# A two-layer decoder trunk on one core: seven-product cases of the last down-projection placed in another order, fed from other buffers, and the end of the last norm written in another order

## The chip, the cores and the metric

The kernel runs on one core of a Trainium2 chip. The metric is the device time of one execution in microseconds (us). Three runs of the kernel before took 2057.11, 2058.33 and 2062.94 us; the median is 2058.33 us.

The engines are named as the profile names them: PE multiplies matrices, PEld is its loading of weights, DVE and ACT do element-wise work, POOL is hardly used here, and SP issues nearly all the transfers (DMAs) from device memory, in order. The chip's memory on the core is 128 partitions wide; a "128x512" tile has 512 numbers of four bytes in each partition. PE sums its products in eight PSUM tiles ("ps", 128x512 each).

## The reference, cut to what matters

Two layers act on 256 tokens of width 2048 (`x`). The change concerns the last step of the second layer, its gated feed-forward network, and the final norm behind it:

```python
D_MODEL, D_FF = 2048, 5632
def conv_ffn(h, w_up, cw, cb, w_down):
    a = h @ w_up                                   # 256 x 2048 by 2048 x 11264
    c = (causal depthwise convolution of width 3 over the tokens of a) + cb
    gate, val = c[..., :D_FF], c[..., D_FF:]
    return (jax.nn.silu(gate) * val) @ w_down      # 256 x 5632 by 5632 x 2048
...
    x = x + conv_ffn(rmsnorm(x, g_ffn[l]), w_ffn_up[l], conv_w[l], conv_b[l], w_ffn_down[l])
return rmsnorm(x, g_final)
```

Everything is in 32-bit floats. `w_down` alone is 5632 x 2048 numbers, 46 MB, and is read once.

## The kernel before, in words

**Two parts for each number.** [...] The high part is a rounded copy (ACT, L702 and L715), the low part is the raw number minus the high one (DVE, L703 and L716). A product of two tiles is three matmuls: high by high, high by low, low by high (`three`, L751 to L753).

**Thirds, halves, cases.** The feed-forward network of layer 1 goes over its 5632 features in thirds of 2048, 2048 and 1536 (`FF_GROUPS = (4, 4, 3)`, in groups of 512). Each third first computes its features (up-projection, convolution, SiLU gate, product) and then multiplies them by its rows of `w_down` and adds the result to the residual stream. That second step, `down_phase`, is where the change lies. It runs twice per third, for the left and the right 1024 columns of the output (`ph` 0 and 1; the text calls them halves). In a half, the work is cut into cases: a case `k` is 256 features, and its weights are two tiles `x` and `y` of 128x1024 floats (512 KB each), loaded by SP (L766). A half has 8 cases in the first two thirds and 6 in the last.

**Plain and seven-product cases.** The output of a half is 256 tokens by 1024 columns, four quarters of 128x512: `e00`, `e01` (first 128 tokens, left and right columns), `e10`, `e11` (second 128 tokens). A plain case adds 8 products (24 matmuls of 128x512) to them. A seven-product case ("fast" in the code) uses sums of its weight quarters and sums of its feature quarters, in the manner of Strassen, and needs 7 products (21 matmuls). Three of them go to `e00`, `e01`, `e10`; four go to accumulators of their own, `m1`, `m5`, `m6`, `m7`, which ACT copies out behind the last such case of a half (`between`, L1332), and which DVE adds into the result later (`combine`, recorded as L1340). The sums of weights are made on DVE: `xs` of 512 columns each (L725, L726, L728, L729) and one low part of 512 (`we`, L722), beside three low parts of 1024 columns (L716). A plain case has two low parts of 1024 (L703) and no sums.

**What sets the order.** `FF_FAST` names the seven-product cases and, for each half, the order of the cases. The order of instructions on PE, DVE and ACT then comes from a scheduler that simulates the program, except in the last half, where `late=2` cases are kept back and the rest is written out by hand (`manual_schedule`). Weight tiles as loaded ("raw") live in a ring of 4 buffers; SP issues a load when the buffer's last reader is done, and the loads behind it wait in SP's queue. High and low parts live in rings too. The eight PSUM tiles of a half are used by the next half once they are read out.

**The end of a half.** `evict(tb, half, ...)` adds the quarter of token block `tb` to the residual `xt` (L1359, DVE). In the last third it also sums the squares (L1375, ACT), multiplies by the gain (L1379, DVE), and behind the last quarter of a token block finishes the norm: small operations on one column (L1381 to L1393), then the scaling of the block's 2048 columns (L1396 on ACT, L1397 and L1398 on DVE), and its output (L1399 to L1401). In the last half the first token block's quarters are evicted, its norm finished and its output issued, all ahead of the second token block's evictions; the very last quarter `e11` goes in two pieces of 256 columns.

Of the kernel before, what the change touches and what calls it, by code (L numbers as in the profile page):

```python
# [34 lines left out]
    4: ((2, 3, 4), ((0, 1, 2, 5, 3, 6, 4, 7), (2, 0, 3, 1, 4, 5, 6, 7))),  # L35
    3: ((1, 2), ((0, 1, 3, 2, 4, 5), (1, 0, 2, 3, 4, 5))),
# [37 lines left out]
class Kernel:  # L74
# [632 lines left out]
    def fast_pair(self, raws, pool):  # L707
# [10 lines left out]

        b21, b22 = parts(y)
# [4 lines left out]
        t13, t24 = sums  # L724
        tt(t13[:, left], x[:, left], x[:, right], ALU.add)  # L725
        tt(t13[:, right], x[:, right], y[:, right], ALU.add)  # L726
        t1, t3 = parts(t13)
        tt(t24[:, left], t13[:, left], y[:, right], ALU.add)  # L728
        tt(t24[:, right], t24[:, left], y[:, left], ALU.add)  # L729
        t2, t4 = parts(t24)  # L730
        return b21, b22, b11, t1, t3, t4, t2


    def down_phase(self, dn, col, order, fast, lhs, rhs, pool, between, evict, late=0):
        mm = self.nc.tensor.matmul
        first_fast = order[0] in fast
        names = ("m1", "m5", "m6", "m7"), ("e00", "e01", "e10", "e11")
        acc = {n: self.psum() for group in (names if first_fast else names[::-1]) for n in group}
# [23 lines left out]
        for n, k in enumerate(order):  # L762
            raws = []
            for i in range(2):
                raw = self.wp.tile([P, 1024], F32, tag="raw", name=self.uid("raw"), bufs=4)
                self.nc.sync.dma_start(out=raw, in_=dn[(2 * k + i) * P : (2 * k + i + 1) * P, col : col + 1024])  # L766
                raws.append(raw)
            if k in fast:
                names7 = "e00", "e01", "m1", "m5", "m7", "e10", "m6"
                for name, q, w in zip(names7, (1, 6, 0, 4, 3, 2, 5), self.fast_pair(raws, pool)):  # L770
# [3 lines left out]
            else:  # L774
# [5 lines left out]
                else:  # L780
                    for half in range(2):
                        plain(k, ws, 0, half)
# [7 lines left out]
        with self.tc.manual_schedule(engines={ET.PE, ET.DVE, ET.Activation}):  # L790
            for half in range(2):
                evict(0, half, acc[f"e0{half}"])
            for k, ws in kept:
                plain(k, ws, 1, 0)
            evict(1, 0, acc["e10"])
            for k, ws in kept[:-1]:
# [8 lines left out]
            evict(1, 1, rest, 1)  # L805


    def ffn(self, l, after=None, to_tokens=None, tokens=None):
# [5 lines left out]
        with self.tc.tile_pool(name=self.uid("ff"), bufs=1) as fp:  # L814
            g0 = 0
            for part, ng in enumerate(FF_GROUPS):
                h = self.ap.tile([P, NB * 512], F32R, tag="big", name=self.uid("h"))
                last = part == len(FF_GROUPS) - 1
                fast, orders = FF_FAST[ng] if tokens is not None else ((), None)
                if tokens is None:  # L820
                    plain = {k: h[:, 1024 * k : 1024 * (k + 1)] for k in range(2 * ng)}
                else:
                    places = [h[:, o : o + 1024] for o in range(1792 * len(fast), NB * 512 - 1023, 1024)]
# [4 lines left out]
                    split7 = {k: h[:, 1792 * i : 1792 * (i + 1)].rearrange("p (s q) -> p s q", s=2) for i, k in enumerate(fast)}  # L828
# [12 lines left out]
                for g in range(g0, g0 + ng):  # L841
# [6 lines left out]
                    def ev(b, acc):  # L848
# [21 lines left out]
                        d = split7[n // 2]  # L870
# [557 lines left out]
```

## Time and profile before

| | |
|---|---|
| median of three runs | 2058.33 us (2057.11 to 2062.94) |
| the profiled execution | 2055.74 us, of which the span of the profile is 2054.0 us |
| PE busy | 2033.3 us, 99% of the span |
| DVE busy | 1508.9 us, 73% |
| ACT busy | 1115.4 us, 54% |
| weight tiles of `w_ffn_down` | 176 transfers of 512 KB (half of them in layer 1) |
| down-projections of layer 1 | 1497 to 1583 us, 1757 to 1843 us, 1974 to 2040 us |

A row of the timeline has the start and the length of an instruction (us), engine, source line, operation, the tile written and the tiles read, and in brackets the idle time ahead of it and what ended it. Matmuls are pipelined: their lengths overlap, and the distance between starts tells the pace. Rows that are merged ("x2") have one start and one total length. In a view of stretches each row has the stretch, its length, the busy time of PE, weight load, DVE, ACT and POOL (with counts), the granted PE clock, the share of the DMA engines and GB/s.

### The profile page before, as it was taken

The page shows a single profiled execution, that of the slowest core. Times are in us where ns is not written, and L with a number is a line of the kernel's source. Part 1 is how long each engine was busy: PE and PEld are TensorE (multiplying, and loading weights), DVE is VectorE, ACT ScalarE, POOL GpSimd, SP SyncE. Part 2 cuts the span into 40 slices and gives each one's busy share as a digit, 9 for nine tenths or more (in the row PEclk, how much of TensorE's full clock was granted, in tenths as well). Part 3 has the DMA queues.
Part 4 walks back from the last instruction along what each step waited for, and adds up shares of the span by engine and source line. Part 5 has one row for each costly group of instructions (what it writes and reads, how often), then busy time and mean ns, then how long its engine had stood idle before and what let it go on. Part 6 is the DMA issues. An engine that isn't in the chain of part 4 may idle for free.

```text
span 2054.0 us, 39946 instructions
## 1 busy us (share of the span) xinstructions
PE 2033.3 (99%) x16226; PEld 1962.6 (96%) x16226; DVE 1508.9 (73%) x2286; ACT 1115.4 (54%) x1613; POOL 142.0 (7%) x200
## 2 busy tenths in 40 slices
PE   9999999999999999999999999999999999999996
PEld 8989999999999999999999999999987999879995
DVE  5866767767656766467788787777787777878788
ACT  6754744555435555345545675455555555555564
POOL 0000013000000000000042242300000000000000
PEclk9999999999999999999999999999999999999999
DMA  8876566666666666666665534668755666566663
GB/s 248 234 215 184 165 194 190 194 194 194 195 195 190 197 194 193 195 195 195 194 191 181 179 119 160 190 199 214 215 192 188 204 195 196 185 196 205 195 210 119
DMA packets 233821, 394.68 MB, mean 192 GB/s; under 512 B 53854, under 2 KB 61348, under 8 KB 233508
## 3 DMA queue, kind: packets, MB, share of 16 engines
q1 hardware_dynamic: 233444, 391.58, 63.4%
q8 instruction: 127, 2.08, 0.4%
q10 hardware_dynamic: 192, 0.54, 0.1%
q14 instruction: 58, 0.48, 0.1%
HBM read 387.88 MB, written 2.10 MB: 190 GB/s over the span
## 4 chain that ended last, share of the span: by engine, by line
PE 90%; DVE 5%; DMA 3%; ACT 1%; issue 1%; DVEq 0%; ACTq 0%; SPq 0%
PE ps L156 25%; PE ps L157 25%; PE ps L159 25%; DMA raw<-in_w_ffn_down 3%; PE ps L188 2%; PE ps L190 2%; PE ps L189 2%; PE ps L752 1%; PE ps L753 1%; PE ps L751 1%; DVE wlo L703 1%; PE ps L523 1%; DVE wlo L716 1%; DVE xs L728 0%; DVE xt L1359 0%
## 5 line engine op out<-in xcount | busy, mean ns | idle before, releaser
L118 DVE TENSOR_TENSOR wlo<-raw,whi 128x1024 fp32r<-128x1024 f32 x572 | 710.3, 1245 | 392.5 <-ACT whi L117 387.8
L117 ACT ACTIVATE whi<-raw 128x1024 fp32r<-128x1024 f32 x572 | 606.5, 1062 | 703.1 <-PE ps L157 591.4
L156 PE MATMUL ps<-xhl,whi 128*128 128x256 f32 x3264 | 762.7, 277 | 0.0
L157 PE MATMUL ps<-xhl,whi 128*128 128x256 f32 x3264 | 761.1, 276 | 0.0
L157 PEld LDWEIGHTS ps<-xhl,whi 128*128 128x128 f32 x3264 | 612.8, 188 | 0.3
L156 PEld LDWEIGHTS ps<-xhl,whi 128*128 128x128 f32 x3264 | 612.7, 188 | 0.3
L159 PE MATMUL ps<-xhl,wlo 128*128 128x256 f32 x3264 | 436.6, 276 | 0.0
L159 PEld LDWEIGHTS ps<-xhl,wlo 128*128 128x128 f32 x3264 | 400.5, 188 | 0.0
L156 PE MATMUL ps<-h,whi 128*128 128x256 f32 x704 | 163.6, 276 | 0.0
L157 PE MATMUL ps<-h,whi 128*128 128x256 f32 x704 | 163.6, 276 | 0.0
L157 PEld LDWEIGHTS ps<-h,whi 128*128 128x128 f32 x704 | 132.0, 188 | 0.0
L156 PEld LDWEIGHTS ps<-h,whi 128*128 128x128 f32 x704 | 131.8, 188 | 0.0
L156 PE MATMUL ps<-mainhl,whi 128*128 128x256 f32 x512 | 119.6, 277 | 0.0
L157 PE MATMUL ps<-mainhl,whi 128*128 128x256 f32 x512 | 119.3, 276 | 0.0
L835 ACT ACTIVATE c<-a,cT 128x256 f32<-128x256 f32 x176 | 99.5, 589 | 9.8 <-DVE a L236 9.7
L157 PEld LDWEIGHTS ps<-mainhl,whi 128*128 128x128 f32 x512 | 96.0, 188 | 0.0
L156 PEld LDWEIGHTS ps<-mainhl,whi 128*128 128x128 f32 x512 | 95.9, 188 | 0.0
L159 PE MATMUL ps<-h,wlo 128*128 128x256 f32 x704 | 94.1, 276 | 0.0
L752 PE MATMUL ps<-wlo,h 128*128 128x512 f32 (+1 forms) x226 | 88.3, 391 | 1.9 <-DVE wlo L703 1.9
L753 PE MATMUL ps<-whi,h 128*128 128x512 f32 (+1 forms) x226 | 87.5, 387 | 0.0
L122 ACT ACTIVATE whi<-raw,gT 128x512 fp32r<-128x512 f32 x96 | 63.9, 716 | 42.2 <-PE ps L157 21.4
L236 DVE TENSOR_TENSOR a<-ps,rbc 128x256 f32<-128x256 f32 x176 | 69.8, 418 | 23.0 <-PE ps L159 23.0
(368 smaller groups left out, 2738.2 us busy)
## 6 DMA issues: line engine op xcount, KB each, us to landing
raw<-in_w_ffn_up SPq DMA_DIRECT2D x352, 512.0 KB, 4.3
raw<-in_w_ffn_down SPq DMA_DIRECT2D x176, 512.0 KB, 4.4
raw<-in_w_out SPq DMA_DIRECT2D x64, 512.0 KB, 4.6
raw<-in_w_in_a SPq DMA_DIRECT2D x56, 512.0 KB, 4.4
raw<-in_w_mem_kv SPq DMA_DIRECT2D x31, 512.0 KB, 4.7
raw<-in_w_in_b SPq DMA_DIRECT2D x16, 512.0 KB, 4.3
raw<-in_w_kv_a SPq DMA_DIRECT2D x9, 512.0 KB, 5.4
raw<-in_w_uq SPq DMA_DIRECT2D x12, 384.0 KB, 3.0
```

The source lines that it names most:

```text
L117: nc.scalar.activation(hi[:, :n], raw[:, :n], AF.Copy)
L118: nc.vector.tensor_tensor(lo[:, :n], raw[:, :n], hi[:, :n].bitcast(F32), ALU.subtract)
L122: nc.scalar.activation(hi[:, s], raw[:, s], AF.Copy, scale=gains[k])
L156: mm(acc[:, :S], wh, x[:, :S], start=first, stop=False)
L157: mm(acc[:, :S], wh, x[:, S:], start=False, stop=False)
L159: mm(acc[:, :S], wl, x[:, :S], start=False, stop=last)
L188: mm(acc, xh, wh, start=first, stop=False)
L189: mm(acc, xh, wl, start=False, stop=False)
L236: self.nc.vector.tensor_tensor(out, acc[:, :S], r, ALU.mult)
L752: mm(o, xh, wl, start=False, stop=False)
L753: mm(o, xl, wh, start=False, stop=stop)
L835: nc.scalar.activation(c, a, AF.Identity, scale=w(2), bias=w(3))
```

## The change

It has six parts, all of them in the down-projection of layer 1's feed-forward network.

1. `FF_FAST`: 15 seven-product cases where there were 16. In the first two thirds the cases 2, 3, 4 stay, and both halves now run in the order 0, 1, 2, 5, 3, 6, 7, 4. In the last third the left half keeps cases 1 and 2 (order 0, 1, 3, 2, 4, 5); the right half has case 1 alone, in the order 0 to 5, and case 2 is a plain case there, whose features come from the quarters that are kept for the left half.
2. Raw tiles: a seven-product case takes its two weight tiles from the ring "gate" of two buffers, which also holds the gate tiles of the up-projection. Only the first seven-product case of each left half and all plain cases take them from the ring "raw" of four.
3. The four sums come first on DVE in a seven-product case, ahead of its low parts.
4. The seven products run in the order `e00, e01, e10, m6, m5, m7, m1` (before: `e00, e01, m1, m5, m7, e10, m6`), and the accumulators are always taken in the order `e` then `m`.
5. The scaling and the output of a token block are a function of their own, `finish`. In the last half `finish(0)` is called behind the eviction of `e10`, the second token block's left quarter.
6. In the last half the two kept cases now bring all their products behind the other cases: both cases' `e00`, eviction, both cases' `e01`, eviction, both cases' `e10`, eviction, then `e11`. Before, `e00` and `e01` of each kept case ran as the case came.

PE has 13705 rows after and 13702 before, DVE 2144 and 2151, ACT 1437 and 1439, SP 769 both.

**DVE where the left half of the first third ends and the right half begins.** `ps_18752` to `ps_18755` are the left half's quarters, whose L1359 (after: L1372) are the evictions. Before, raw_19176 and raw_19178 are the weights of the right half's case 3, wlo_19116 belongs to its case 2, and wlo_19145 to its plain case 0:

```order
L725 TENSOR_TENSOR xs_19180<-raw_19176 128x512
L716 TENSOR_TENSOR wlo_19116<-xs_19099,whi_19115 128x1024
L1359 TENSOR_TENSOR xt<-ps_18752,xt 128x512
L722 TENSOR_TENSOR we_19186<-raw_19176,we_19186 128x512
L726 TENSOR_TENSOR xs_19180<-raw_19176,raw_19178 128x512
L1359 TENSOR_TENSOR xt<-ps_18753,xt 128x512
L728 TENSOR_TENSOR xs_19181<-xs_19180,raw_19178 128x512
L1359 TENSOR_TENSOR xt<-ps_18754,xt 128x512
L1359 TENSOR_TENSOR xt<-ps_18755,xt 128x512
L703 TENSOR_TENSOR wlo_19145<-raw_19140,whi_19144 128x1024
```

After, gate_19166 and gate_19168 are the weights of the right half's case 2, wlo_19054 is the last low part of the left half's case 4, and wlo_19099 and wlo_19103 are those of the right half's first case, the plain case 0:

```order
L716 TENSOR_TENSOR wlo_19054<-xs_19036,whi_19053 128x1024
L721 TENSOR_TENSOR xs_19170<-gate_19166,gate_19168 128x512
L1372 TENSOR_TENSOR xt<-ps_18755,xt 128x512
L722 TENSOR_TENSOR xs_19171<-xs_19170,gate_19168 128x512
L1372 TENSOR_TENSOR xt<-ps_18752,xt 128x512
L703 TENSOR_TENSOR wlo_19099<-raw_19094,whi_19098 128x1024
L1372 TENSOR_TENSOR xt<-ps_18753,xt 128x512
L1372 TENSOR_TENSOR xt<-ps_18754,xt 128x512
L723 TENSOR_TENSOR xs_19171<-xs_19171,gate_19168 128x512
L703 TENSOR_TENSOR wlo_19103<-raw_19096,whi_19102 128x1024
```

The half now begins with a plain case, and two sums of a later case stand between the last low part of one half and the first of the next.

**SP's queue in the left half of the last third.** The names 24110 and 24112 are case 3, 24146 and 24148 case 2, 24196 and 24198 case 4, 24232 and 24234 case 5; higher numbers belong to the right half. Before:

```order
L766 DMA raw_24110<-in_w_ffn_down 128x1024
L766 DMA raw_24112<-in_w_ffn_down 128x1024
L766 DMA raw_24146<-in_w_ffn_down 128x1024
L766 DMA raw_24148<-in_w_ffn_down 128x1024
L766 DMA raw_24196<-in_w_ffn_down 128x1024
L766 DMA raw_24198<-in_w_ffn_down 128x1024
L766 DMA raw_24232<-in_w_ffn_down 128x1024
L766 DMA raw_24234<-in_w_ffn_down 128x1024
```

After (case 2's first tile, gate_24146, stands earlier, out of this piece):

```order
L768 DMA raw_24110<-in_w_ffn_down 128x1024
L768 DMA raw_24112<-in_w_ffn_down 128x1024
L768 DMA raw_24196<-in_w_ffn_down 128x1024
L768 DMA raw_24198<-in_w_ffn_down 128x1024
L768 DMA raw_24232<-in_w_ffn_down 128x1024
L768 DMA raw_24234<-in_w_ffn_down 128x1024
L768 DMA gate_24148<-in_w_ffn_down 128x1024
L768 DMA gate_24334<-in_w_ffn_down 128x1024
```

Case 2's second tile has moved behind the tiles of the cases 4 and 5, which run after it.

**DVE around case 2 of that half, after.** gate_23460 is the last gate tile of the up-projection, whose last reader is L863 (before: L854), and gate_24148 takes its buffer; L245 is the low part of the features:

```order
L727 TENSOR_TENSOR we_24160<-gate_24146,we_24160 128x512
L863 TENSOR_TENSOR hv_24013<-gate_23460,c_24009 128x256
L245 TENSOR_TENSOR h_22333<-hv_24013,h_22333 128x256
L721 TENSOR_TENSOR xs_24150<-gate_24146,gate_24148 128x512
L722 TENSOR_TENSOR xs_24151<-xs_24150,gate_24148 128x512
L716 TENSOR_TENSOR wlo_24157<-gate_24148,whi_24156 128x1024
```

The load of gate_24148 now comes between the second row and the fourth.

**DVE in the last half's end.** Before, `ps_24295` is the first token block's second quarter, `ps_24296` and `ps_24297` are the second token block's quarters:

```order
L1359 TENSOR_TENSOR xt<-ps_24295,xt 128x512
L1387 TENSOR_SCALAR fv<-fsums,fpart 128x1
L1391 RECIPROCAL froot<-froot 128x1
L1392 SCALAR_TENSOR_TENSOR fq<-froot,fv 128x1
L1393 SCALAR_TENSOR_TENSOR froot<-fq,froot 128x1
L1397 TENSOR_SCALAR xt<-xt,froot 128x512
L1398 SCALAR_TENSOR_TENSOR xt<-xt,froot,gb 128x512
L1359 TENSOR_TENSOR xt<-ps_24296,xt 128x512
L1379 TENSOR_TENSOR xt<-xt,gb 128x512
L1381 TENSOR_REDUCE fpart<-fsums 128x1
L1382 TENSOR_SCALAR fpart<-fpart 128x1
L1359 TENSOR_TENSOR xt<-ps_24297,xt 128x256 x2
```

After (`ps_24291`, `ps_24292`, `ps_24293` are the same three):

```order
L1372 TENSOR_TENSOR xt<-ps_24291,xt 128x512
L1400 TENSOR_SCALAR fv<-fsums,fpart 128x1
L1404 RECIPROCAL froot<-froot 128x1
L1405 SCALAR_TENSOR_TENSOR fq<-froot,fv 128x1
L1406 SCALAR_TENSOR_TENSOR froot<-fq,froot 128x1
L1372 TENSOR_TENSOR xt<-ps_24292,xt 128x512
L1392 TENSOR_TENSOR xt<-xt,gb 128x512
L1394 TENSOR_REDUCE fpart<-fsums 128x1
L1395 TENSOR_SCALAR fpart<-fpart 128x1
L1412 TENSOR_SCALAR xt<-xt,froot 128x512
L1413 SCALAR_TENSOR_TENSOR xt<-xt,froot,gb 128x512
L1372 TENSOR_TENSOR xt<-ps_24293,xt 128x256 x2
```

The two scalings of the first block have moved behind the second block's first quarter.

The diff, cut to its core:

```diff
 FF_FAST = {
-    4: ((2, 3, 4), ((0, 1, 2, 5, 3, 6, 4, 7), (2, 0, 3, 1, 4, 5, 6, 7))),
-    3: ((1, 2), ((0, 1, 3, 2, 4, 5), (1, 0, 2, 3, 4, 5))),
+    4: (((2, 3, 4), (0, 1, 2, 5, 3, 6, 7, 4)), ((2, 3, 4), (0, 1, 2, 5, 3, 6, 7, 4))),
+    3: (((1, 2), (0, 1, 3, 2, 4, 5)), ((1,), (0, 1, 2, 3, 4, 5))),
 }
...
+        t13, t24 = sums
+        tt(t13[:, left], x[:, left], x[:, right], ALU.add)
+        tt(t13[:, right], x[:, right], y[:, right], ALU.add)
+        tt(t24[:, left], t13[:, left], y[:, right], ALU.add)
+        tt(t24[:, right], t24[:, left], y[:, left], ALU.add)
         b21, b22 = parts(y)
         one = self.tmp(pool, [P, 1040], "we", 1, F32R)[:, :1024]
...
-        t13, t24 = sums
-        tt(t13[:, left], x[:, left], x[:, right], ALU.add)
-        tt(t13[:, right], x[:, right], y[:, right], ALU.add)
+        t2, t4 = parts(t24)
         t1, t3 = parts(t13)
-        tt(t24[:, left], t13[:, left], y[:, right], ALU.add)
-        tt(t24[:, right], t24[:, left], y[:, left], ALU.add)
-        t2, t4 = parts(t24)
-        return b21, b22, b11, t1, t3, t4, t2
+        return b21, b22, t4, t2, t1, t3, b11
...
-        first_fast = order[0] in fast
-        acc = {n: self.psum() for group in (names if first_fast else names[::-1]) for n in group}
+        acc = {n: self.psum() for group in names[::-1] for n in group}
...
-                raw = self.wp.tile([P, 1024], F32, tag="raw", name=self.uid("raw"), bufs=4)
+                if k in fast and (col or k != fast[0]):
+                    raw = self.tmp(fp, [P, 1024], "gate", 2)
+                else:
+                    raw = self.wp.tile([P, 1024], F32, tag="raw", name=self.uid("raw"), bufs=4)
...
-                names7 = "e00", "e01", "m1", "m5", "m7", "e10", "m6"
-                for name, q, w in zip(names7, (1, 6, 0, 4, 3, 2, 5), self.fast_pair(raws, pool)):
+                names7 = "e00", "e01", "e10", "m6", "m5", "m7", "m1"
+                for name, q, w in zip(names7, (1, 6, 2, 5, 4, 3, 0), self.fast_pair(raws, pool)):
...
                 else:
-                    for half in range(2):
-                        plain(k, ws, 0, half)
                     kept.append((k, ws))
...
             for half in range(2):
+                for k, ws in kept:
+                    plain(k, ws, 0, half)
                 evict(0, half, acc[f"e0{half}"])
             for k, ws in kept:
                 plain(k, ws, 1, 0)
             evict(1, 0, acc["e10"])
+            finish(0)
...
             evict(1, 1, rest, 1)
+            finish(1)
...
-            y, rows = xt[:, tb, :], slice(tb * P, (tb + 1) * P)
-            for a in (512, 1024):
-                nc.scalar.activation(y[:, a : a + 512], y[:, a : a + 512], AF.Copy, scale=one(r))
+
+    def finish(self, tb):
+        nc, y, rows, r = self.nc, self.xt[:, tb, :], slice(tb * P, (tb + 1) * P), self.r[:, tb : tb + 1]
+        for a in (512, 1024):
+            nc.scalar.activation(y[:, a : a + 512], y[:, a : a + 512], AF.Copy, scale=r)
```

What is left out of the diff: the features of the last third's case 2, which stay whole there (1024 columns of quarters where a seven-product case keeps 896) so that the right half can use them as a plain case; and the rest of `finish`, which is the old end of `evict` as it was.

36 lines of the change are left out of this document (22 added, 14 removed).

## Prediction

> **What bounds the kernel now.** I read the page first (busy shares, chain), then the stretches of the three down-projections, then PE's waits, then the timeline where the longest waits lie.
>
> ```profile
> span 2054.0 us, 39946 instructions
> PE 2033.3 (99%) x16226; PEld 1962.6 (96%) x16226; DVE 1508.9 (73%) x2286; ACT 1115.4 (54%) x1613; POOL 142.0 (7%) x200
> PE 90%; DVE 5%; DMA 3%; ACT 1%; issue 1%; DVEq 0%; ACTq 0%; SPq 0%
> ```
>
> PE is busy for 99%: the time is PE's matmuls, its few waits, and what lies behind the last matmul. Ahead of the first down-projection nothing is changed.
>
> ```profile
> 1496.93:1583.31 86.38, 84.43 (x369) 68.31 (x368) 71.86 (x92) 47.70 (x59) 0.00 (x0) 1.00 0.59 191
> 1757.40:1842.94 85.54, 84.38 (x369) 68.32 (x367) 71.94 (x92) 47.93 (x59) 0.00 (x0) 1.00 0.58 192
> 1973.51:2040.26 66.75, 64.41 (x284) 51.60 (x282) 62.27 (x86) 38.92 (x57) 0.00 (x0) 1.00 0.43 141
> ...
> 1567.15 0.91 PE ps L751 x4
> ...
> 2040.02 0.28 PE L752 MATMUL ps<-wlo,h 128*128 128x256 f32 x1
> 2040.14 0.28 PE L753 MATMUL ps<-whi,h 128*128 128x256 f32 x1
> ```
>
> A 128x512 matmul takes 0.91/4 = 0.2267 us, a 256-wide one 2040.14 - 2040.02 = 0.12 us. A third has 6x21 + 10x24 = 366 matmuls, 82.97 us without a wait, so the first two stretches hold 3.4 and 2.6 us of waits; the last has 270 wide and 12 narrow ones, 62.65 us, so 4.1 us. In all 10.1 us, and behind the last matmul 2054.0 - 2040.14 = 13.86 us. These two sums are all that the change can take from, beside the matmuls themselves.
>
> ```profile
> PE ps L751 <- DVE xt L1359: 1.9, 2, 1.2
> PE ps L752 <- DVE wlo L703: 1.9, 4, 0.6
> PE ps L751 <- ACT staged L1332: 0.7, 1, 0.7
> PE ps L751 <- ACT whi L715: 0.7, 2, 0.5
> PE ps L751 <- ACT whi L702: 0.3, 1, 0.3
> ```
>
> PE waits for DVE most: for evictions (L1359) and low parts (L703). DVE is 72 of 86 us busy in a stretch, so it has slack but is late in places.
>
> **The matmuls.** One seven-product case less: 24 - 21 = 3 matmuls, +0.68 us, all on the path. DVE loses one case's four sums and `we`, less than it has to spare; the plain case's features come from the quarters that exist, so ACT and DVE copy 128 columns more, which lies under the up-projection's matmuls. The new order of the sums inside a case moves no work between engines.
>
> **The border between halves, first two thirds.**
>
> ```profile
> 1541.15 0.39 PE L751 MATMUL ps<-we,h 128*128 128x512 f32 x1
> 1542.79 0.50 PE L751 MATMUL ps<-whi,h 128*128 128x512 f32 x1 [1.24 <-DVE xt L1359]
> ...
> 1540.30 0.69 DVE L725 TENSOR_TENSOR xs<-raw 128x512 f32<-128x512 f32 x1 [2.79 <-DMA raw<-in_w_ffn_down]
> 1542.05 0.68 DVE L1359 TENSOR_TENSOR xt<-ps,xt 128x512 f32<-128x512 f32 x1
> 1545.05 1.28 DVE L1359 TENSOR_TENSOR xt<-ps,xt 128x512 f32<-128x512 f32 x2
> 1546.25 2.35 DVE L703 TENSOR_TENSOR wlo<-raw,whi 128x1024 fp32r<-128x1024 f32 x2
> ```
>
> PE stands still before 1542.79 because an eviction at 1542.05 is late; it stands in DVE's queue behind L725, which waited 2.79 us for a raw tile. This wait goes: the right half now begins with two plain cases, and its first seven-product case has buffers of its own. What is late next: the order of after puts, between the left half's last low part and the right half's first, two sums and two evictions, 4 x 0.6 us (start of L1359 to start of L703 here: 1.20 for two), then the low part, 1.13 us (2.35 less overlap, for two): 3.6 us. In that time PE has the last low part's remaining products, about 8 matmuls, 1.8 us. So PE waits 1.8 us, restarts cost about 0.1 each (the row of 0.50 in place of 0.39), and case 4, now last with its sums and evictions close, about 0.9 later in the half: 3.2 us in a third, 6.4 for both, against 3.4 + 2.6 = 6.0. Term: +0.4. Ends: -4 (the sums slip into idle time, no border wait: 1.8 x 2 and restarts) and +4 (DVE starts none of the 3.6 us ahead of PE's need).
>
> **Case 2 of the last third's left half.** Its second tile is moved in SP's queue behind the tiles of cases 4 and 5 and takes the buffer of the last gate tile, which is free when L854 has read it.
>
> ```profile
> 1985.35 0.68 DVE L729 TENSOR_TENSOR xs<-xs,raw 128x512 f32<-128x512 f32 x1
> 1985.95 1.22 DVE L703 TENSOR_TENSOR wlo<-raw,whi 128x1024 fp32r<-128x1024 f32 x1
> ...
> 1988.41 1.22 DVE L716 TENSOR_TENSOR wlo<-raw,whi 128x1024 fp32r<-128x1024 f32 x1
> 1990.68 0.42 DVE L854 TENSOR_TENSOR hv<-gate,c 128x256 f32<-128x256 f32 x1
> ...
> 1989.86 0.61 PE L751 MATMUL ps<-whi,h 128*128 128x512 f32 x2
> ...
> raw<-in_w_ffn_down SPq DMA_DIRECT2D x176, 512.0 KB, 4.4
> ...
> L702 ACT ACTIVATE whi<-raw 128x1024 fp32r<-128x1024 f32 x55 | 57.4, 1055 | 22.2 <-PE ps L157 8.0 <-PE ps L753 5.9 <-DMA raw<-in_w_ffn_down 3.7
> ```
>
> The last L854 ran at 1990.68, with case 2's sums and low parts ahead of it. After, these can't be, since their tile comes later: three sums at 0.6 and two low parts at 1.13 are 4.1 us, less some 0.4 of idle time and a low part of features ahead of it: the product ends near 1987.0. The load takes 4.4 us, to 1991.4; the high part 1.06, to 1992.5. PE needs it at 1989.86: it waits 2.6 us. Then the case runs at DVE's pace: low part of `y` to 1993.6 (PE waits 0.9 after one matmul), third sum and high part of `t24` to 1995.3 (0.5 to 0.8), its low part to 1996.4 (0.9). PE has done 12 matmuls at 1997.6 in place of 1989.86 + 12 x 0.2267 = 1992.6: 5.0 us. Behind it the order has two sums of the right half's case 1 ahead of case 4's low part: 0.9 more; restarts 0.5: 6.4 us. For the rest of the stretch I keep 1.2 us, since the right half has one seven-product case and most of DVE's slack: 7.6 us against 4.1. Term: +3.5. Queued behind the held load on SP are the tiles of the right half's case 1 alone, needed some 11 us later, so nobody else waits. Ends: +1 (the product is done 1 us sooner and the load takes 3.2) and +6 (it isn't done sooner than 1988 and the load takes 5).
>
> **The end.**
>
> ```profile
> 2036.77 0.69 DVE L1359 TENSOR_TENSOR xt<-ps,xt 128x512 f32<-128x512 f32 x1 [1.22 <-PE ps L753]
> ...
> 2039.11 0.68 DVE L1359 TENSOR_TENSOR xt<-ps,xt 128x512 f32<-128x512 f32 x1
> ...
> 2041.71 0.49 DVE L1397 TENSOR_SCALAR xt<-xt,froot 128x512 f32<-128x512 f32 x1
> 2042.11 0.75 DVE L1398 SCALAR_TENSOR_TENSOR xt<-xt,froot,gb 128x512 f32<-128x512 f32 x1
> 2042.78 0.68 DVE L1359 TENSOR_TENSOR xt<-ps,xt 128x512 f32<-128x512 f32 x1
> ...
> 2045.11 0.74 DVE L1359 TENSOR_TENSOR xt<-ps,xt 128x256 f32<-128x256 f32 x2
> ...
> 2046.74 0.48 DVE L1371 CUSTOM_DVE_ANT_0 fjunk<-xt,fpart 128x256 f32<-128x256 f32 x1
> ...
> 2049.57 0.38 ACTq L1401 DMA_DIRECT2D out_y<-xt  x1
> ```
>
> With E for the last matmul's start, 2040.14: the last sum of squares is at E + 6.6, and from there to the end it is 7.26 us, 4.4 of them the last output. DVE takes the first quarter at E - 3.4 and the second block's first at E + 2.64 only, although PE finished it before E: the first block's chain, with L1397 and L1398, stands ahead. After, a quarter's two kept cases are 12 matmuls, 2.7 us; `e11` has 6 x 0.2267 + 12 x 0.12 = 2.8. So `e10` is done at E - 2.8, `e01` at E - 5.5, `e00` at E - 8.2, and DVE takes each as it comes: `e10` at E - 2.35 and its small work to E - 0.0 (2.33 us, 2042.78 to 2045.11 here), then the first block's scaling to E + 1.05 (1.07 us, 2041.71 to 2042.78), then the last quarter's pieces (1.63 us, 2045.11 to 2046.74): the last sum of squares at E + 2.7 in place of E + 6.6. Term: -3.9. Ends: -4.5 (scaling done while DVE would wait) and -2 (the first block's output, now nearer to the second's, holds it up).
>
> **The sum.** +0.68 + 0.4 + 3.5 - 3.9 = +0.7. The profiled execution took 2055.74 us, 1.74 of them around the span, and is 2.6 us below the median of the runs. On the median: 2058.33 + 0.7 = 2059.0 us.
>
> **Rivals.**
>
> *A hidden load, a quiet border (faster).*
>
> ```profile
> L725 DVE TENSOR_TENSOR xs<-raw 128x512 f32<-128x512 f32 x16 | 11.1, 691 | 12.3 <-DMA raw<-in_w_ffn_down 12.3
> ```
>
> Two buffers of their own let SP fetch a seven-product case's tiles without waiting for the plain ring; now DVE waits 12.3 us for them ahead of L725, which speaks for it. If the borders' waits go (6.0 to 2.4) and case 2 is no later than now: 0.68 - 3.6 + 0 - 3.9 = -6.8, 2051.5 us. Against it: the buffer of case 2's tile is held by L854, as the order shows.
>
> *The two buffers hold up every half (slower).* A seven-product case's load is issued only when the last such case's tiles are read, and the plain tiles queue behind it on SP.
>
> ```profile
> SPq L766 <- DVE hv L854: 14.9, 3, 7.2
> ```
>
> SP already waits up to 7.2 us on such a hold. From one such case to the next with a plain case between, PE has 5.44 + 4.76 = 10.2 us; load and DVE's work on the next (4.4 + 3 x 1.13 + 5 x 0.6 = 10.8) don't quite fit if DVE has no lead. Should both right halves pay half of case 2's price, 3.2 us each, it is +7.1, 2065.5 us; at the full price +13.5, 2072 us. It decides from a lead of DVE under 0.6 us; now DVE has idle time of 14 us in a stretch, which speaks against it.
>
> *The tail's gain doesn't come.* If DVE is late at E by the same amount (its combine, 1.13 a piece, ahead of the evictions), the sum without the last term is +4.6: 2062.9 us.
>
> *The clock.*
>
> ```profile
> 2043.00:2044.00 1.00, 0.00 (x0) 0.00 (x0) 0.46 (x1) 0.55 (x2) 0.00 (x0) 1.00 0.92 342
> 2044.00:2045.00 1.00, 0.00 (x0) 0.00 (x0) 0.75 (x2) 0.22 (x2) 0.00 (x0) 0.54 1.05 412
> ```
>
> Behind the last matmul PE's granted clock stays 1.00 until about 2044, 3.5 us or so after PE fell idle, then goes to 0.5. The wait of 2.6 us at case 2 is shorter. If the load comes 1 us later, PE idles that long, and runs its next matmuls at half pace; for how long no row shows. If the return takes the same 3.5 us it costs 1.7, and with the longer wait +2.7: 2061.7 us; at once, +1.0: 2060.0 us. [...]
>
> **The numbers.** Forecast 0.60, hidden load 0.10, buffers hold up halves 0.17, tail without gain 0.08, clock 0.05. A measurement of this kernel can tell about 0.3% (6.2 us) from no change: the three runs lie 0.28% apart. The forecast, the tail and the clock lie within that. Faster takes 0.08 of the hidden load and 0.02 from the forecast's low ends; slower takes 0.14 of the held halves, the rest of which costs less, and 0.03 from the high ends of the others: faster 0.10, same 0.73, slower 0.17. The range is 2053 to 2066. Below, the border at -4 and case 2 at +1 together give +0.7 - 4.4 - 2.5 = -6.2, 2052.1 us, drawn in by 0.9 since both must happen. Above, the held halves at half price end at 2065.5. Outside lie most of the hidden load and the held halves at more than half price, some 0.2.
>
> **What would show it.** The first two stretches about as long as now, with the border wait on L703 (after) in place of the eviction; in the last stretch PE's longest wait near 1990 on the high part of case 2's second tile, and that tile's load issued behind the last gate product; the last sum of squares 2.7 us behind the last matmul in place of 6.6. The forecast is wrong if that load lands before 1989, if waits of over 1 us show in the middle of the right halves, or if the evictions of the last half come late behind the combine.

## The result, and the profile after

The changed kernel took 2055.67 us in the median of 11 runs (2052.82 to 2059.72); the kernel before, 2059.33 us in 11 runs beside it (2057.11 to 2062.94). The ratio is 0.9982, 95% interval 0.9972 to 0.9991: 3.7 us less, with an interval from 1.9 to 5.8 us. A second comparison gave 0.9988 (0.9980 to 0.9996). The time lies in the forecast's range and within 0.3%, but the sign is the other one: a small gain, where 0.7 us more was forecast.

The two profiles say the opposite at first sight: the profiled execution of after took 2056.95 us, that of before 2055.74 us. The page of after, in the same three lines (its size, its engines, the chain by engine):

```profile
span 2055.2 us, 39936 instructions
PE 2034.6 (99%) x16229; PEld 1962.0 (95%) x16229; DVE 1503.4 (73%) x2280; ACT 1114.7 (54%) x1611; POOL 142.0 (7%) x200
...
PE 88%; DVE 6%; DMA 4%; issue 1%; ACT 1%; SPq 0%; DVEq 0%; ACTq 0%
```

The view of stretches, for the three down-projections of after:

```profile
1496.42:1582.89 86.47, 84.88 (x372) 68.79 (x371) 71.81 (x94) 48.42 (x58) 0.00 (x0) 1.00 0.53 177
1756.57:1843.47 86.90, 85.06 (x372) 68.71 (x371) 71.67 (x94) 48.13 (x58) 0.00 (x0) 1.00 0.53 176
1973.63:2045.52 71.89, 66.59 (x287) 52.86 (x285) 60.73 (x89) 39.37 (x61) 0.00 (x0) 0.98 0.38 127
```

The first two are as long as before or a little longer, the last 5 us longer, with a mean clock of 0.98. PE's waits from 1490 us on:

```profile
PE ps L750 <- ACT whi L715: 3.6, 1, 3.6
PE ps L751 <- DVE wlo L716: 2.7, 3, 1.2
PE ps L751 <- DVE wlo L703: 2.4, 7, 0.7
```

The evictions are gone from this list. In their place stand one wait of 3.6 us on a high part and waits on low parts. The end of the timeline, PE's last matmul and DVE's rows behind it:

```profile
2045.40 0.28 PE L752 MATMUL ps<-whi,h 128*128 128x256 f32 x1
...
2042.93 0.69 DVE L1372 TENSOR_TENSOR xt<-ps,xt 128x512 f32<-128x512 f32 x1
2045.28 0.48 DVE L1412 TENSOR_SCALAR xt<-xt,froot 128x512 f32<-128x512 f32 x1
2046.33 0.75 DVE L1372 TENSOR_TENSOR xt<-ps,xt 128x256 f32<-128x256 f32 x2
2047.97 0.48 DVE L1384 CUSTOM_DVE_ANT_0 fjunk<-xt,fpart 128x256 f32<-128x256 f32 x1
```

The last sum of squares comes 2.57 us behind the last matmul in place of 6.60, and the span ends 9.83 us behind it in place of 13.84.

So the profiles, piece by piece, put after at +1.2 us, and eleven runs of each put it at -3.7. The profiled execution of before, 2055.74 us, lies below all eleven of its runs; that of after lies above the median of its own. So the two can't be set against each other as they are. What a usual execution of either looks like was the first thing to find out.

### The profile page after: what moved, and what is told of

The parts are those of the page before. It is cut to its first block, busy times and chain, and to the rows that moved or that the text cites. A ratio compares the mean times of both kernels' runs of the same rounds, so it can differ in the third digit from the quotient of the medians.

```text
span 2055.2 us, 39936 instructions
## 1 busy us (share of the span) xinstructions
PE 2034.6 (99%) x16229; PEld 1962.0 (95%) x16229; DVE 1503.4 (73%) x2280; ACT 1114.7 (54%) x1611; POOL 142.0 (7%) x200
## 4 chain that ended last, share of the span: by engine, by line
PE 88%; DVE 6%; DMA 4%; issue 1%; ACT 1%; SPq 0%; DVEq 0%; ACTq 0%
PE ps L156 25%; PE ps L157 25%; PE ps L159 25%; DMA gate<-in_w_ffn_down 3%; PE ps L188 2%; PE ps L189 2%; PE ps L190 2%; DVE wlo L703 2%; DMA raw<-in_w_ffn_down 1%; DVE wlo L716 1%; PE ps L523 1%; PE ps L751 1%; PE ps L752 1%; PE ps L750 1%; DVE xs L722 0%
## 5 line engine op out<-in xcount | busy, mean ns | idle before, releaser
L123 DVE SCALAR_TENSOR_TENSOR wlo<-raw,gT,whi 128x512 fp32r<-128x512 f32 x96 | 72.2, 789 | 22.0 <-ACT whi L122 21.9
```

What stands on the lines that cost most here:

```text
L123: nc.vector.scalar_tensor_tensor(lo[:, s], raw[:, s], gains[k], hi[:, s].bitcast(F32), ALU.mult, ALU.subtract)
```

## The experiments

All times below are against runs of the kernel before on the same chip, with 5 to 12 executions of each kernel. The table has them together; the stretches are from the start of the first to the start of the last matmul of each down-projection, read from the trace of each run's one profiled execution, and "end" is from there to the end of the span. Without any wait the first two are 82.7 us (365 x 0.2267). In kernels with the new order four matmuls of the next up-projection run between the last ones of a stretch, so 83.2 us is the bound there; the up-projection behind is 0.42 us shorter in turn (173.90 and 130.38 us in place of 174.32 and 130.80, the same in every profile).

| run | first | second | last | end | ratio (interval) | median us |
|---|---|---|---|---|---|---|
| before | 86.15 | 85.31 | 66.63 | 13.84 | | |
| before again | 87.04 | 86.47 | 67.77 | 13.88 | 1.0004 (0.9995 to 1.0012) | 2058.62 |
| after | 86.24 | 86.68 | 71.78 | 9.83 | 0.9982 (0.9972 to 0.9991) | 2055.67 |
| after again | 86.99 | 86.88 | 71.10 | 9.79 | 0.9988 (0.9980 to 0.9996) | 2055.62 |
| end alone | 87.80 | 85.92 | 72.62 | 9.80 | 0.9999 (0.9990 to 1.0008) | 2058.55 |
| first two thirds alone | 86.43 | 85.75 | 67.47 | 13.87 | 0.9986 (0.9977 to 0.9994) | 2054.97 |
| last third alone | 86.61 | 85.57 | 71.40 | 9.82 | 0.9998 (0.9989 to 1.0007) | 2056.80 |
| first two thirds, plain ring | 83.66 | 83.83 | 68.33 | 13.84 | 0.9973 (0.9961 to 0.9984) | 2051.43 |
| orders alone | 83.24 | 83.39 | 71.15 | 13.87 | 0.9968 (0.9955 to 0.9980) | 2052.15 |
| sums alone | 84.66 | 85.23 | 68.44 | 13.85 | 0.9982 (0.9973 to 0.9991) | 2054.75 |
| case 2 on the plain ring | 84.07 | 84.36 | 66.38 | 9.82 | 0.9956 (0.9944 to 0.9968) | 2050.03 |
| the same with 16 cases | 86.60 | 87.16 | 68.16 | 12.19 | 0.9980 (0.9971 to 0.9988) | 2053.64 |
| plain ring but one case | 83.24 | 83.71 | 66.28 | 9.79 | 0.9936 (0.9924 to 0.9949) | 2045.07 |
| plain ring throughout | 84.86 | 83.69 | 67.87 | 9.81 | 0.9947 (0.9935 to 0.9960) | 2047.84 |

**Both kernels again, unchanged.**

> The kernel before, unchanged, for a second profile. Its profile on record is a quick execution (2055.74 us, below all eleven other runs, median 2059.33), that of after a slow one (2056.95, median 2055.67), so the profiles put after 1.2 us later and the medians 3.7 us earlier. Theory S (the missing microseconds are in the down-projections: a usual execution of before waits longer there): the three stretches, 86.15, 85.31 and 66.63 us in the profile on record, are together 3 to 5 us longer here. Theory U (they are in stretches that the change leaves alone, 1496.93, 174.32 and 130.80 us): those are together 3 to 4 us longer, the three down-projections within 1 us of the record, and the change itself costs about 2.6 us in its own stretches. Time against before: the same, within 0.1%.

> The kernel after, unchanged, for a second profile and a second interval. Both theories: 0.9982 of before, within 0.9970 to 0.9995. Theory S: down-projections of 86.2, 86.7 and 71.8 us within 1 us in total. Theory U: these may come out shorter, and the stretches outside 1 to 2 us shorter or longer. The wait at case 2 of the last third's left half should be seen again (3.73 us at 1993.70 in the first profile), the matmuls behind it at 0.43 us in place of 0.23 if the clock falls again; from the last matmul's start to the end 9.8 us.

The second profile of before has the longer stretches that Theory S asked for: 0.89, 1.16 and 1.14 us more, 3.2 in all, and nothing moved in the up-projections. The second profile of after repeats the first: the same three stretches within 1 us, a wait of 2.9 us at case 2 with slow matmuls behind it, and an end of 9.79 us. (The part ahead of 1497 us varies by 2 us either way, in kernels where nothing differs there: it started the first down-projection at 1495.4 here, at 1497.6 in the second profile of after.) PE's waits in the first two thirds of the second profile of before:

```profile
PE ps L752 <- DVE wlo L703: 2.5, 6, 0.5
PE ps L751 <- DVE xt L1359: 2.1, 2, 1.3
```

Four profiles share before's program in the first two thirds (before twice, the end alone, the last third alone): their waits there are 6.0, 8.0, 8.2 and 6.7 us, 7.2 in the mean. The profile that the forecast was made from has the least. (These are the stretches less the 165.5 us without a wait, 166.3 in the new order. The lists of waits show about half as much: behind each wait the first two matmuls start some 0.28 us late in all, and short waits aren't listed.) Five share after's (after twice, the first two thirds alone, case 2 on the plain ring, the same with 16 cases): 6.6, 7.5, 5.9, 2.1 and 7.4 us, 5.9 in the mean. In the last third six profiles share before's program (before twice, the first two thirds alone, and the three runs on parts of those, below): the stretch takes from 66.6 to 71.2 us, 68.3 in the mean, and again the profile of the forecast has the least. One profile of either kernel can't carry a sum of a few microseconds here.

**The end alone** (parts 5 and 6).

```diff
                 else:
-                    for half in range(2):
-                        plain(k, ws, 0, half)
                     kept.append((k, ws))
...
             for half in range(2):
+                for k, ws in kept:
+                    plain(k, ws, 0, half)
                 evict(0, half, acc[f"e0{half}"])
...
             evict(1, 0, acc["e10"])
+            finish(0)
```

> Before with the parts 5 and 6 of the change alone (the finish of the first token block behind the second block's first eviction, and both kept cases quarter by quarter). Forecast's term: -3.9 us, from 13.84 us behind the last matmul to 9.9; ratio 0.9981. If PE waits in the last half grow, because both kept cases' low parts are now needed together (rival): the last down-projection longer than 66.63 by 1 to 2 us, -2 us in all, ratio 0.9990.

The end is 9.80 us, as asked, but the last stretch is 72.62 us, 5.4 us longer than in the mean of before's two profiles (67.2) and 4.3 longer than in the mean of all six profiles with before's last third (68.3); the time is that of before. The rival was right, and dearer than put. PE's waits in that stretch, and two pieces of it:

```profile
PE ps L752 <- DVE wlo L703: 3.9, 4, 1.8
...
2034.00:2038.00 4.00, 1.89 (x6) 1.16 (x7) 4.00 (x5) 0.90 (x1) 0.00 (x0) 1.00 0.00 0
2038.00:2042.00 4.00, 4.00 (x12) 3.11 (x11) 1.81 (x5) 2.21 (x4) 0.00 (x0) 0.57 0.01 4
```

DVE is full (4.00 of 4.00 us) with low parts and the additions of the seven-product sums. In the old order PE has other products to do meanwhile: in before's profile it has no wait behind 2024.7. In the new one both kept cases' low parts are wanted for `e00` alone, and PE stands. And behind that wait the granted clock is 0.57.

**Case 2 on the plain ring.**

```diff
-                if k in fast and (col or k != fast[0]):
+                if k in fast and (col or k != fast[0]) and (col or len(order) > 6):
```

> After, but the last third's left half takes case 2's two tiles from the plain ring of four, so that its second tile is loaded in the order of use and waits for no gate tile. If the held load is the cause of the wait at case 2: the wait of 3.73 us and the slow matmuls behind it go, the last down-projection is 66 to 68 us in place of 71.78, the time 4 to 5 us below after, ratio to before 0.996. If the plain ring is then late by as much (rival): 70 us or more, ratio 0.998.

The wait at case 2 goes, with what followed it: 66.38 us in place of 71.78 and 71.10, and 5.6 us less than after in the medians. All that PE still waits for in this stretch:

```profile
PE ps L751 <- DVE wlo L703: 1.6, 3, 1.1
```

The held load was the cause. In after the place reads (DVE, then PE, then two pieces of a microsecond):

```profile
1986.69 0.42 DVE L863 TENSOR_TENSOR hv<-gate,c 128x256 f32<-128x256 f32 x1
1992.59 0.69 DVE L721 TENSOR_TENSOR xs<-gate,gate 128x512 f32<-128x512 f32 x1 [4.57 <-DMA gate<-in_w_ffn_down]
...
1993.70 0.73 PE L750 MATMUL ps<-whi,h 128*128 128x512 f32 x2 [3.56 <-ACT whi L715]
1995.07 0.79 PE L751 MATMUL ps<-wlo,h 128*128 128x512 f32 x1 [0.64 <-DVE wlo L716]
...
1996.00:1997.00 1.00, 1.00 (x4) 0.50 (x3) 0.19 (x1) 1.00 (x2) 0.00 (x0) 0.50 0.34 53
1998.00:1999.00 1.00, 1.00 (x6) 0.83 (x6) 1.00 (x2) 1.00 (x2) 0.00 (x0) 0.94 0.50 201
```

The last gate tile is read by 1987.1, the load lands 5.5 us later, the high part is done at 1993.6. Four matmuls touch the first microsecond where six are usual: PE ran at half clock from 1994.7 to 1998.1, which cost 1.6 us by the distances between starts.

**The first two thirds alone, and the last third alone.** In either, the other part is that of before, instruction by instruction.

```diff
+        new = len(order) > 6        # the last third alone: len(order) == 6
...
-                if k in fast and (col or k != fast[0]):
+                if new and k in fast and (col or k != fast[0]):
...
+                names7 = ("e00", "e01", "e10", "m6", "m5", "m7", "m1") if new else ("e00", "e01", "m1", "m5", "m7", "e10", "m6")
```

> The change in the first two thirds alone (orders, own tiles, sums first, products in the new order); the last third and the end as before. The forecast's term for this is +0.4 us, ratio 1.0002. Theory F (the forecast missed a gain at the borders between halves, and the rest of its sum was right): -2.5 to -3.5 us, ratio 0.9985, the two stretches together 2 to 4 us shorter than in the profiles of before (171.5 and 173.5 us), the evictions gone from PE's waits. Theory L (the gain missed lies in the last third): 1.000.

> The change in the last third and the end alone; the first two thirds as before. The forecast's terms for this are +0.68 + 3.5 - 3.9 = +0.3 us, ratio 1.0001, and both profiles of after say the same (last stretch 71.4 us in the mean against 67.2, end 9.8 against 13.9: +0.1). Theory F: 1.000, within 0.0008. Theory L: 0.9985, with the wait at case 2 shorter in most executions than in the two profiles.

Theory F: the first two thirds carry the gain, -2.9 us (0.9986), the last third and the end nothing that can be told (0.9998, -0.4 us with an interval from -2.3 to +1.4), and together they are what the whole change gave. But the stretches of this profile, 172.2 us for both (171.3 without the eight matmuls moved in), are not 2 to 4 us below before's 171.5 and 173.5, as the theory had asked; the gain is seen in the times alone. What it is made of the next three runs tell.

**The plain ring, the orders, the sums, in the first two thirds.** The first is the run with the first two thirds alone, without own tiles; the others have the new case orders alone, or the new sums and products alone, both on the plain ring and with the old last third.

```diff
-                if new and k in fast and (col or k != fast[0]):
+                if False and k in fast and (col or k != fast[0]):
...
# the sums alone keep the orders of the "-" line; the orders alone: new = False, and
-    4: (((2, 3, 4), (0, 1, 2, 5, 3, 6, 4, 7)), ((2, 3, 4), (2, 0, 3, 1, 4, 5, 6, 7))),
+    4: (((2, 3, 4), (0, 1, 2, 5, 3, 6, 7, 4)), ((2, 3, 4), (0, 1, 2, 5, 3, 6, 7, 4))),
```

> As the run with the first two thirds alone, but with all weight tiles from the plain ring of four: orders, sums and products are new, the tiles are not. If own tiles carry the gain (Theory T): 2 to 4 us more than with them, ratio 1.000 or above, and DVE's waits for tiles as long as before (12.3 us ahead of the first sum over all halves). If order and sums carry it: the same as with own tiles within 1 us.

> In the first two thirds the new case orders alone (two plain cases first in the right half too, two between the cases 3 and 4), with the sums, the products and the tile ring of before; the last third and the end as before. If the spacing carries the gain: 0.9975 and the two stretches 83.5 to 84.5 us; if the order of the sums does: 0.999 to 1.000, waits on low parts in place of the eviction.

> In the first two thirds the four sums first and the products in the new order, with the case orders and the tile ring of before; the last third and the end as before. Of the 5.6 us that new orders and new sums gained together with the plain ring (0.9973): if the spacing carries it, this gives 0.999 to 1.000 and the right halves, which begin with case 2, still wait for an eviction behind a late tile; if the order of the sums carries it, 0.9975.

The orders alone give 0.9968, 6.6 us, and in its profile PE waits for nothing in the first two thirds: 83.24 and 83.39 us, against a bound of 83.2. In the view of stretches PE is busy for the whole length of both:

```profile
1495.71:1579.18 83.47, 83.47 (x372) 69.17 (x371) 72.18 (x93) 48.49 (x58) 0.00 (x0) 1.00 0.57 189
1752.86:1836.47 83.61, 83.61 (x372) 69.02 (x371) 71.33 (x92) 48.30 (x58) 0.00 (x0) 1.00 0.58 189
```

The sums alone give somewhat more than half as much (0.9982), and together they give no more than the orders; the intervals of the three overlap, so how the gain divides isn't settled. The expectation for the sums alone was wrong: the time lies between its two cases, and the eviction is no longer waited for, though the right halves still begin with case 2. All that PE waits for in the first two thirds of that run:

```profile
PE ps L767 <- DVE wlo L703: 2.8, 4, 1.0
```

With own tiles on top of orders and sums, part of the gain is lost again: 0.9986 against 0.9973. These intervals overlap, too, but six of the seven executions without own tiles are quicker than all eleven with them. The rows of groups of instructions for the first two sums, DVE in the first two thirds, of after and of the run with the plain ring (the wait for tiles is the last number):

```profile
L721 DVE TENSOR_TENSOR xs<-gate,gate 128x512 f32<-128x512 f32 x10 | 6.9, 691 | 5.8 <-DMA gate<-in_w_ffn_down 5.7
L720 DVE TENSOR_TENSOR xs<-gate 128x512 f32<-128x512 f32 x10 | 6.9, 688 | 9.0 <-DMA gate<-in_w_ffn_down 8.9
L720 DVE TENSOR_TENSOR xs<-raw 128x512 f32<-128x512 f32 x2 | 1.4, 692 | 3.6 <-DMA raw<-in_w_ffn_down 3.6
L721 DVE TENSOR_TENSOR xs<-raw,raw 128x512 f32<-128x512 f32 x2 | 1.4, 688 | 0.3 <-DMA raw<-in_w_ffn_down 0.3
```

```profile
L735 DVE TENSOR_TENSOR xs<-raw,raw 128x512 f32<-128x512 f32 x12 | 8.3, 693 | 8.2 <-DMA raw<-in_w_ffn_down 8.2
L734 DVE TENSOR_TENSOR xs<-raw 128x512 f32<-128x512 f32 x12 | 8.3, 689 | 5.5 <-DMA raw<-in_w_ffn_down 5.4
```

With the two cases of after that still take plain tiles, it is 18.5 us in after and 13.6 with the plain ring: own tiles do not shorten DVE's waiting, as Theory T would have had it, but lengthen it. What PE feels of it depends on where it falls. In after, behind case 3 of the first third's right half (DVE, then PE):

```profile
1557.43 1.22 DVE L716 TENSOR_TENSOR wlo<-xs,whi 128x1024 fp32r<-128x1024 f32 x1
1563.28 0.69 DVE L720 TENSOR_TENSOR xs<-gate 128x512 f32<-128x512 f32 x1 [4.63 <-DMA gate<-in_w_ffn_down]
1563.88 1.22 DVE L716 TENSOR_TENSOR wlo<-xs,whi 128x1024 fp32r<-128x1024 f32 x1
...
1565.16 0.50 PE L751 MATMUL ps<-wlo,h 128*128 128x512 f32 x1 [1.18 <-DVE wlo L716]
```

The scheduler put the first sum of case 4 (1563.28) ahead of the last low part of case 3 (1563.88). With two buffers, case 4's load goes out only when case 3's tiles are read, near 1557.5, and takes 5.8 us; DVE stands on the sum for 4.63 us, and the low part behind it in the queue is what PE waits for.

In the profile with the orders alone the clock falls in the last third, too, 1.2 us behind a wait of 1.74 us, and a second wait, of 0.69 us, lies inside the slow stretch:

```profile
2004.49 0.50 PE L767 MATMUL ps<-wlo,h 128*128 128x512 f32 x1 [1.74 <-DVE wlo L703]
2008.01 0.79 PE L766 MATMUL ps<-whi,h 128*128 128x512 f32 x1 [0.69 <-ACT staged L1362]
...
2006.00:2007.00 1.00, 1.00 (x4) 0.50 (x2) 1.00 (x2) 0.00 (x0) 0.00 (x0) 0.50 0.93 352
2008.00:2012.00 4.00, 3.99 (x9) 3.14 (x10) 4.00 (x6) 0.00 (x0) 0.00 (x0) 0.50 0.67 219
```

That is why its last stretch is 71.15 us with before's program; the run with the plain ring has the same two waits at the same place (1.72 and 0.69) and keeps its clock at 1.00; the last section comes back to this.

**Sixteen cases.**

```diff
-    3: (((1, 2), (0, 1, 3, 2, 4, 5)), ((1,), (0, 1, 2, 3, 4, 5))),
+    3: (((1, 2), (0, 1, 3, 2, 4, 5)), ((1, 2), (0, 1, 3, 2, 4, 5))),
```

> After with case 2 of the last third's left half from the plain ring (which gave 0.9956), and with 16 seven-product cases: the last right half has the cases 1 and 2, in the order 0, 1, 3, 2, 4, 5. Three matmuls less: -0.68 us if DVE has room, ratio 0.9953. If the fifteenth case was dropped for DVE's sake (its four sums, a low part of 512 and one of 1024 more, 4.2 us, and the combine beside them): the end of the last stretch waits 1 to 4 us more, ratio 0.996 to 0.9975, PE's waits there on low parts.

Three matmuls less, and 3.6 us more than with fifteen cases in the medians. The last stretch is 1.8 us longer and the end 2.4 us (12.19 against 9.82): DVE is late with low parts and with the first block's eviction. In the first two thirds the programs are the same, and what the profiles differ by there (5.3 us) is chance; these 4.2 us are in the part that differs. Doing without the sixteenth case is what pays for the new end; the end alone, with sixteen, gained nothing.

**Without own tiles.** The last two join what gained: the plain ring for all tiles but those of case 1 in the last right half, and the plain ring throughout.

```diff
-                if k in fast and (col or k != fast[0]):
+                if k in fast and col and len(order) == 6:        # throughout: if False:
```

> After, with the plain ring for all weight tiles but those of case 1 in the last right half. It joins the two runs that gained by giving up own tiles: first two thirds as in the run with the plain ring (0.9973 with the old last third), last third as in the run with case 2 on the plain ring (0.9956 with own tiles in the first two). If own tiles cost what these runs say, 2.7 us in the first two thirds and 5.1 us at case 2: 2.7 us below the latter, 0.9943 to 0.9950, 2047 us; stretches 83.7, 83.8 and 66.4 us, the end 9.8. If the 0.9956 already had the gain of quick loads (its profile had 84.07 and 84.36 us where after has 86.2 to 87.0): no better than 0.9956.

> After with no own tiles at all. As the run with own tiles for case 1 of the last right half alone, within 1 us, if those two loads, asked for long before their use, matter to nobody; 1 to 2 us more if they keep the right half's plain tiles in time.

The first is the quickest kernel of all: 2045.07 us, 0.9936 (0.9924 to 0.9949), some 13 us below before and 10 below after. Its waits in the three down-projections:

```profile
PE ps L751 <- DVE wlo L703: 1.3, 2, 1.1
PE ps L750 <- ACT whi L702: 0.4, 1, 0.4
```

It is better than case 2 on the plain ring alone (0.9956) by about 4 us. The two intervals overlap, but the pair without the new last third (0.9973 against 0.9986) says the same, so own tiles do cost some 3 to 4 us in the first two thirds. And without the held load the new last third gains on its own: stretch and end together take 76.1 us here and 76.2 with case 2 on the plain ring, against 80.5 to 85.0 (82.2 in the mean) in the six profiles with before's last third. Giving up the last case's own tiles as well is 2.8 us dearer in the medians (0.9947), again with intervals that overlap; its profile has waits on low parts (L716) of 2.4 us in all that the better kernel's has not. Why that one case does well with tiles of its own was not tried further.

## Why the prediction was wrong, step by step

**The matmuls, +0.68:** three more, at the pace put. (0.91/4 is 0.2275 and not 0.2267, but 0.2267 is what the runs have: it makes the 83.2 us that the orders alone reach.) What was left out is DVE's side of it: one case less gives DVE the room that the new end needs. The forecast said that DVE had more than enough to spare; in the last right half it had none (4.00 us busy of 4.00 from 2034 on, in the run with the end alone).

**The border between halves, +0.4: this step failed.** The measured effect of everything in the first two thirds is -2.9 us (from -4.7 to -1.2). Two things were wrong in it, the wait of after at the border and the waits of before that it was set against. First, "PE has the last low part's remaining products, about 8 matmuls, 1.8 us", which made a wait of 1.8 us. That takes PE to be at that low part when DVE finishes it. In after the border reads (DVE, then PE):

```profile
1533.63 1.23 DVE L716 TENSOR_TENSOR wlo<-xs,whi 128x1024 fp32r<-128x1024 f32 x1 [0.94 <-ACT whi L715]
1538.17 1.22 DVE L703 TENSOR_TENSOR wlo<-raw,whi 128x1024 fp32r<-128x1024 f32 x1
...
1539.44 0.50 PE L751 MATMUL ps<-wlo,h 128*128 128x512 f32 x1
```

DVE did much as forecast (4.5 us from the end of one low part to the end of the next, 0.9 of them a wait for a tile, where 3.6 were put), but when it had finished the first one, at 1534.86, PE still had some 20 matmuls, 4.5 us, and stood for 0.1. So the wait of 1.8 us at the border does not come. The lead that DVE has there had to be counted; with the orders alone there is no wait left at all. That the 6.4 us of waits expected for after were about right (6.6 and 7.5 in its two profiles, 5.9 in the mean of five) is luck: they stand later, in the second part of either half, and go with the own tiles. The forecast's own sign of being wrong, a wait of over 1 us in the middle of a right half, is the 1.18 us at 1565.16. Second, the waits of before, 6.0 us, were taken from a quick execution: 7.2 us is the mean of four. The 2.6 us between that execution and the median was carried along as a constant offset (against the eleven runs it is 3.6); 1.2 us of it are these very waits, and 1.7 us lie in the last third (68.3 us in the mean in place of 66.6). The profiles thus give 5.9 - 7.2 = -1.3 us for the first two thirds; that lies just within the interval of the runs, and the rest of the -2.9 isn't traced to a place.

**Case 2, +3.5:** right in place and cause; in size, too, on the side of after. The forecast had 7.6 us of waits in after's last stretch, and its two profiles have 8.6 and 7.9. But the 4.1 us of before that these were set against were again those of a quick execution: the six profiles with before's last third have 5.8 in the mean, so the term is nearer +2.5 than +3.5. Inside the sum three things moved: the gate product was done at 1987.1 (1987.0 put), the load took 5.5 us (4.4 put), so PE waited 3.73 us by the distance between starts (2.6 put), and behind it the clock was halved, which took the place of the later waits on DVE.

**The end, -3.9:** right: -4.0 in every profile with the new order and fifteen cases. It is worth its time in after because the sixteenth seven-product case is gone, which the forecast did not see; as an edit alone it gains nothing.

**The rivals.** The quiet border came, as the hidden load rival had it, but from orders and sums, and not from own tiles, whose loads aren't hidden. The rival of the two buffers came too, at 2.7 us by the ratios (0.9986 against 0.9973) in place of 6.4 and more. The clock came, with the late load that it asked for, at 1.6 us (1.7 put). That sum's return after 3.5 us was the author's estimate, which no row of before shows; in after the half clock lasted 3.4 us. The forecast had these against each other as separate cases; in the kernel they are all there at once, and the one that was missed, the orders' 6 us, is the largest.

## What to carry to other kernels

Before a stall is costed, read how far the producer is ahead at that place: count the consumer's instructions between the two, and not only what a moved row adds. A separate small ring for some loads is no gain by itself: with two buffers a load goes out when the last user is done, and a scheduler that puts the next load's first reader ahead of work already due turns the load's time into a wait for everything behind it (here, behind a load of 5.8 us, 4.63 us for DVE and 1.18 us for PE). And where single microseconds decide, look at several profiles of the kernel before; the stretch that a change removes may be the one that varies.

## What had not been expected of the hardware

The clock of PE fell to half (0.50, with 0.43 us from one matmul's start to the next in place of 0.23) not only after waits as long as the 3.5 us that the end of before's profile had suggested, as after 3.56 us in after (half clock from 1994.7 to 1998.1, 3.4 us, 1.6 us lost), but also after 0.52 and 1.76 us in the run with the end alone (from 2038.5 to 2042.0, 3.4 us), and after 1.74 us with the orders alone, where it stayed at half from 2005.7 to 2012.5, 6.8 us (these ends are worked out from the mean clock of pieces of 0.5 and 1 us). With the plain ring a wait of 1.72 us at the same place, and one of 0.69 us behind it as with the orders alone, left it at 1.00. The views of both, the orders alone first:

```profile
2000.00:2004.00 4.00, 2.75 (x13) 1.94 (x11) 4.00 (x6) 2.85 (x5) 0.00 (x0) 1.00 0.12 47
2004.00:2008.00 4.00, 2.83 (x8) 1.71 (x8) 4.00 (x6) 1.00 (x2) 0.00 (x0) 0.71 0.51 178
```

```profile
2004.00:2008.00 4.00, 2.11 (x8) 1.43 (x8) 4.00 (x6) 1.77 (x4) 0.00 (x0) 1.00 0.37 131
2008.00:2012.00 4.00, 3.82 (x17) 3.17 (x18) 4.00 (x6) 0.13 (x1) 0.00 (x0) 1.00 0.73 237
```

So in these runs the length of one wait doesn't tell whether the clock falls: 1.74 us had the half clock behind it, 1.72 us had not. What makes the difference is not shown.

The time from the issue of a 512 KB tile to its landing was 5.5 and 5.8 us in the two waits shown, where the page of before has a median of 4.4; the same program's waits in the first two thirds ran from 2.1 to 7.5 us between executions. What makes a load slow in one execution and not in another stays open.
